# Two-layer decoder trunk on one core: another order for the loads at the start, for the memory attention's projections and for the branch inputs of the merge

## The chip, the cores and the metric

The kernel runs on one core of a Trainium2 chip. The metric is device microseconds of one execution. Before the change three runs took 1638.13, 1638.89 and 1640.25 us; the median is 1638.89 us. One further execution was profiled.

## The reference, cut to what matters

The program computes two layers of a post-norm decoder on x (1024 tokens by 1024 channels, float32). In each layer one projection of x feeds four token mixers, each mixer is gated and projected, and the four are merged. In short form:

```python
h = x @ w_in
(c_q, c_kv, k_rope, sb_qkv, fox_qkv, fox_f, mem_q, gate_z, merge_r) = _split_last(h, IN_SPLITS)
q  = (_rms_norm(c_q, q_norm) @ w_qb)            # branch 0: latent attention with rotary part
kv = (_rms_norm(c_kv, kv_norm) @ w_kvb)
y_mla = causal_softmax(q, kv)
y_sb  = stick_breaking(sb_qkv)                  # branch 1
y_fox = causal_softmax(fox_qkv, log_decay)      # branch 2
mk, mv = jnp.split(mem @ w_mem_kv, 2, axis=-1)  # branch 3: 256 memory tokens
y_mem = softmax((mem_q / 8) @ mk.T) @ mv
merge_g = sigmoid(merge_r @ w_merge_up)
for n in range(4):
    yb = branches[n] * silu(gate_z[:, :, n])
    merged = merged + merge_g[:, :, n] * (yb @ w_branch[n])
x = layer_norm(ALPHA * x + merged @ w_out)
```

## The kernel before, in words

**Numbers in two parts.** Every operand of a large product is split in a high part (float32r) and the rest, its low part, and a product is three matmuls: high by high, low by high, high by low (`passes`, L235 to L237). So each tensor that TensorE reads has a step ahead of it in which one engine writes the high part and another the low part. For activations that is `split_evac`: ScalarE copies (L145, with a scale L148) and VectorE subtracts (L146, with a scale L149). For weights it is `split_pool` on GpSimd (L154 and L157). A tile is 128 by 512, and a projection of the 1024 tokens is done in two halves of 512.

**Weights.** `Stream` takes blocks of 128 by 128 out of one long array in the order that `weight_blocks` lays down; four blocks are one DMA (`wr`, three buffers) and one pair of split tiles (`wh`, `wl`, four buffers each).

**Operands of attention.** `stack_pair` writes a projection's result for two heads into two tiles, opA and opB: ScalarE writes half of opA from PSUM, VectorE the other half out of PSUM and that half (L281, L282), and then the same for opB.

**Order.** The Python code is one program, and a scheduler of the framework puts each engine's instructions in an order of its own, with a simulated timeline. `after(later, earlier)` (L118) only pins an order. Each engine then runs its list strictly in that order, and so does SyncE (SP), which issues the loads. PSUM tiles come from three pools; four banks (`PJ`) serve the projections, and a projection waits until the reader of the bank's last result is done.

**Stages around the change.** At the start of layer 0, x arrives transposed: eight tiles `xr` for the first half of the tokens, taking turns with eight `wAr`, then small tensors, then eight `xr` for the second half. The first product (`pA`, 292 columns: the latent, the rotary key and the forget gate) runs over 8 blocks of tokens. After the first three attentions comes the memory stage: `mem_prep` loads mem, splits it (`memh`, `meml`) and projects keys and values (`mk`, `mv`, matmuls of 256 columns) for two pairs of heads, woven with `cq_norm` (sums of squares for the norm of c_q, `ssp`, L747); then comes the query projection of pair 0. In the gate and latent stage the last gates are projected (`last_gates`), the merge input mr is split (`split_mr`), the gated output of branch 2 is split (`split_y`, tiles `ybh` and `ybl`), the norm weights for q are loaded (`load_wq`), and the latent is transposed (`ckT`), split (`ckTh`, `ckTl`) and projected to keys (`mla_k`) and values (`mla_v`). There `main` holds this list of steps, and `early` feeds in the first steps of the merge (`pg`, `pb`, `mg`, `acc`).

## Time and profile before

| | us |
|---|---|
| median of three runs | 1638.89 |
| profiled execution | 1637.25 |
| its span in the profile | 1635.5 |
| TensorE matmul (PE) busy | 1577.1 (96%) |
| VectorE (DVE) busy | 1057.4 (65%) |
| ScalarE (ACT) busy | 739.4 (45%) |
| GpSimd (POOL) busy | 828.3 (51%) |

PE is busy nearly all the time, and the others about half. So what counts is where PE waits, and where its granted clock is half: the mean granted clock is 0.986 of full. In a row of a timeline, "[1.71 <-DVE xTl L146]" says that the engine stood idle for 1.71 us before this instruction and that VectorE's write of xTl at line 146 ended it. A stretch of a table by windows has, per engine, its busy time and in brackets how many instructions touched it. PEclk is the granted clock, 1.00 for 2.4 GHz and 0.50 for 1.2 GHz.

### The profile page before, as it was taken

The page shows a single profiled execution, that of the slowest core. Times are in us where ns is not written, and L with a number is a line of the kernel's source. Part 1 is how long each engine was busy: PE and PEld are TensorE (multiplying, and loading weights), DVE is VectorE, ACT ScalarE, POOL GpSimd, SP SyncE. Part 2 cuts the span into 40 slices and gives each one's busy share as a digit, 9 for nine tenths or more (in the row PEclk, how much of TensorE's full clock was granted, in tenths as well). Part 3 has the DMA queues.
Part 4 walks back from the last instruction along what each step waited for, and adds up shares of the span by engine and source line. Part 5 has one row for each costly group of instructions (what it writes and reads, how often), then busy time and mean ns, then how long its engine had stood idle before and what let it go on. Part 6 is the DMA issues. An engine that isn't in the chain of part 4 may idle for free. (4 is left out here: it accounts for less than half of the span.)

```text
span 1635.5 us, 24787 instructions
## 1 busy us (share of the span) xinstructions
PE 1577.1 (96%) x8454; PEld 1338.6 (82%) x8454; DVE 1057.4 (65%) x2053; ACT 739.4 (45%) x1632; POOL 828.3 (51%) x971
## 2 busy tenths in 40 slices
PE   9999999999999999989899999999999999999995
PEld 8888888888878888868798888888888788887784
DVE  6456699734436789962673567997343467899618
ACT  4355655534434656420333556655343346564202
POOL 5775535665462344454446664356564623355325
PEclk9999999999999999999899999999999999999998
DMA  5312112232242222132212221122322412221213
GB/s 178 110 56 62 42 36 71 78 88 64 82 127 65 69 71 78 46 116 93 108 68 91 62 59 49 36 64 78 94 66 80 134 56 72 62 84 53 96 65 115
DMA packets 84333, 127.92 MB, mean 78 GB/s; under 512 B 13232, under 2 KB 38640, under 8 KB 84208
## 3 DMA queue, kind: packets, MB, share of 16 engines
q1 hardware_dynamic: 84208, 126.34, 24.9%
q8 instruction: 67, 1.10, 0.3%
q14 instruction: 58, 0.48, 0.1%
HBM read 89.57 MB, written 19.96 MB: 67 GB/s over the span
## 5 line engine op out<-in xcount | busy, mean ns | idle before, releaser
L235 PE MATMUL pj<-xTh,wh 128*128 128x512 f32 x832 | 330.1, 397 | 2.2 <-DVE mx L399 1.4
L237 PE MATMUL pj<-xTh,wl 128*128 128x512 f32 x832 | 326.3, 393 | 0.0
L236 PE MATMUL pj<-xTl,wh 128*128 128x512 f32 x832 | 325.9, 392 | 0.0
L154 POOL TENSOR_SCALAR wh<-wr 128x512 fp32r<-128x512 f32 x168 | 113.9, 678 | 234.5 <-PE pj L236 104.1
L157 POOL TENSOR_TENSOR wl<-wr,wh 128x512 fp32r<-128x512 f32 x168 | 227.1, 1353 | 9.8
L146 DVE TENSOR_TENSOR pl<-pt,ph 128x384 fp32r<-128x384 f32 (+1 forms) x272 | 170.7, 639 | 70.7 <-ACT ph L145 68.3
L145 ACT CAST ph<-pt 128x384 fp32r<-128x384 f32 (+1 forms) x272 | 146.4, 551 | 132.8 <-PE pt L430 128.1
L411 POOL TENSOR_SCALAR p<-p,sm 128x896 f32<-128x896 f32 (+7 forms) x128 | 102.2, 799 | 169.7 <-DVE sm L410 169.3
L237 PEld LDWEIGHTS pj<-xTh,wl 128*128 128x128 f32 x832 | 156.3, 188 | 32.1
L235 PEld LDWEIGHTS pj<-xTh,wh 128*128 128x128 f32 x832 | 156.6, 188 | 29.0 <-DVE mx L399 1.8
L236 PEld LDWEIGHTS pj<-xTl,wh 128*128 128x128 f32 x832 | 156.5, 188 | 26.0
L125 ACT ACTIVATE p<-p,mx 128x896 f32<-128x896 f32 (+7 forms) x128 | 99.4, 777 | 66.9 <-DVE mx L399 57.6
L460 PE MATMUL y<-pl,v 128*128 128x256 f32 (+1 forms) x544 | 121.4, 303 | 0.0
L460 PE MATMUL y<-ph,v 128*128 128x256 f32 (+1 forms) x544 | 111.4, 283 | 1.8 <-ACT ph L145 1.7
L235 PE MATMUL pb<-ybh,wh 128*128 128x512 f32 x256 | 104.3, 407 | 9.0 <-DVE mg L1041 5.4
L430 PE MATMUL pt<-ident_r,p 128*128 128x128 f32 x704 | 110.7, 273 | 0.0
L125 ACT ACTIVATE mg<-pg 128x512 f32<-128x512 f32 x128 | 76.2, 595 | 65.6 <-PE pg L237 40.1
L460 PEld LDWEIGHTS y<-ph,v 128*128 128x128 f32 x544 | 93.2, 189 | 15.0 <-ACT ph L145 3.0
L404 DVE TENSOR_TENSOR_SCAN kt<-kt,unseen 128x896 f32<-128x896 f32 (+3 forms) x64 | 98.0, 1543 | 10.0 <-ACT kt L125 9.8
L237 PE MATMUL po<-woh,mgl 128*128 128x512 f32 x256 | 100.8, 395 | 0.0
L391 POOL TENSOR_SCALAR_AFFINE_SELECT bt<-bt 128x128 f32<-128x128 f32 x64 | 53.0, 831 | 94.1 <-ACT bt L125 85.2
L236 PE MATMUL po<-wol,mgh 128*128 128x512 f32 x256 | 100.5, 396 | 0.0
(266 smaller groups left out, 3692.2 us busy)
## 6 DMA issues: line engine op xcount, KB each, us to landing
wr<-in_w_s_dram SPq DMA_DIRECT2D x168, 256.0 KB, 2.6
s<-opA SPq DMA_DIRECT2D x128, 64.0 KB, 2.0
s<-opB SPq DMA_DIRECT2D x128, 64.0 KB, 2.0
wr<-in_w_out_dram SPq DMA_DIRECT2D x32, 256.0 KB, 2.6
xr<-in_x_t_dram SPq DMA_DIRECT2D x16, 256.0 KB, 5.3
ckb<-c_d SPq DMA_DIRECT2D x8, 512.0 KB, 3.8
y_d<-y SPq DMA_DIRECT2D x16, 256.0 KB, 2.0
y<-y_d SPq DMA_DIRECT2D x16, 256.0 KB, 3.6
```

What stands on the lines that cost most here:

```text
L125: i = act.activation(*args, **kw)
L145: act.copy(h, src)
L146: return dve.tensor_tensor(l, src, f(h), ALU.subtract)
L154: i = pool.tensor_scalar(h, src, 1.0, 1.0, ALU.mult, ALU.mult)
L157: pool.tensor_tensor(l, src, f(h), ALU.subtract)
L235: pe.matmul(ps, ah, bh, start=k == 0, stop=False)
L236: pe.matmul(ps, ah, bl, start=False, stop=False)
L237: pe.matmul(ps, al, bh, start=False, stop=k == nk - 1)
L404: dve.tensor_tensor_scan(kt[:, ::-1], kt[:, ::-1], unseen[:, S - w:][:, ::-1], 1.0, ALU.mult, ALU.max)
L411: pool.tensor_scalar(p, p, sm, 1.0, ALU.mult, ALU.mult)
L430: pe.transpose(pt[:, c:c + P], self.p[i][:, b * P:(b + 1) * P], ident)
L460: pe.matmul(u.y[:, q0 * P:256], u.op["v"][b][:, u.head, :], src[:, s * 256 + q0 * P:s * 256 + 256], start=j == 0 and n == 0, stop=j == n_c ...
```

## The change

Four edits. At the start, the small loads and the first four weight tiles are pinned behind the last load of the second half of x. In the memory stage, the query projection of pair 0 goes first, with the splits of mem and the sums of squares woven in, and the memory's keys and values follow; the weight array has its blocks in the new order. The merge input is split straight out of PSUM when it is projected, and no longer copied and split later. In the latent stage the splits of branch 2 and the load of q's weights are steps of `main` between the latent's and the keys' projections.

```diff
--- before.py
+++ after.py
@@ -196,6 +196,7 @@
         dve.tensor_tensor(dst, dst, t, ALU.mult)
 
     xT = {}
+    last_load = [None]
 
 
     def transpose_x(half, tiles):
@@ -211,7 +212,9 @@
     def wload(n):
 
         raw = rp.tile([P, HALF], F32, tag="wr", name=nm("wr"))
-        nc.sync.dma_start(raw, w_s[n])
+        i = nc.sync.dma_start(raw, w_s[n])
+        if n < 4:
+            after(i, last_load[0])
         wh = hp.tile([P, HALF], F32R, tag="wh", name=nm("wh"))
         wl = hp.tile([P, HALF], F32R, tag="wl", name=nm("wl"))
         split_pool(raw, wh, wl)
@@ -526,7 +529,7 @@
     def load_x(half, k):
 
         raw = U("xr", F32)
-        nc.sync.dma_start(raw, x_t[k * P:(k + 1) * P, half * HALF:(half + 1) * HALF])
+        last_load[0] = nc.sync.dma_start(raw, x_t[k * P:(k + 1) * P, half * HALF:(half + 1) * HALF])
         return raw
 
     def split_x(half, k, raw):
@@ -572,7 +575,7 @@
 
 
     pos_i = cp.tile([P, NB], I32, name="pos_i")
-    nc.sync.dma_start(pos_i, positions.rearrange("o (b p) -> p (o b)", p=P), allow_slow_non_contiguous=True)
+    after(nc.sync.dma_start(pos_i, positions.rearrange("o (b p) -> p (o b)", p=P), allow_slow_non_contiguous=True), last_load[0])
     pos_f = cp.tile([P, NB], F32, name="pos_f")
     inv = cp.tile([P, 16], F32, name="inv")
     freqs = (10000.0 ** (-np.arange(0, ROPE, 2, dtype=np.float64) / ROPE)).astype(np.float32)
@@ -635,7 +638,7 @@
 
 
         fb = tp.tile([P, 4], F32, tag="fb", name=nm("fb"), bufs=1)
-        nc.sync.dma_start(fb, fox_forget_bias[layer].partition_broadcast(P))
+        after(nc.sync.dma_start(fb, fox_forget_bias[layer].partition_broadcast(P)), last_load[0])
         for h in range(4):
             dve.tensor_scalar(fn[:, :, h], fn[:, :, h], fb[:, h:h + 1], 1.0, ALU.add, ALU.mult)
         lf = tp.tile([P, NB, 4], F32, tag="lf", name=nm("lf"), bufs=1)
@@ -713,14 +716,15 @@
         mr = [None, None]
 
         def evac_mr(ps, half):
-            mr[half] = U("mr", F32)
-            act.copy(mr[half], ps)
+            h, l = U("mrh"), U("mrl")
+            split_evac(ps, h, l)
+            mr[half] = (h, l)
 
 
         gq = tp.tile([P, 3], F32, tag="gq", name=nm("gq"), bufs=1)
         gk = tp.tile([P, 2], F32, tag="gk", name=nm("gk"), bufs=1)
-        nc.sync.dma_start(gq, mla_q_norm[layer].rearrange("(k p) -> p k", p=P), allow_slow_non_contiguous=True)
-        nc.sync.dma_start(gk, mla_kv_norm[layer].rearrange("(k p) -> p k", p=P), allow_slow_non_contiguous=True)
+        for g, src in ((gq, mla_q_norm), (gk, mla_kv_norm)):
+            after(nc.sync.dma_start(g, src[layer].rearrange("(k p) -> p k", p=P), allow_slow_non_contiguous=True), last_load[0])
 
         sq = [None, None]
         rq = tp.tile([P, NB], F32, tag="rq", name=nm("rq"), bufs=1)
@@ -745,6 +749,7 @@
             ps = PT("ssp")
             for b in range(NB):
                 pe.matmul(ps[:, 2 * b:2 * b + 1], sq[b // 4][:, (b % 4) * P:(b % 4) * P + P], ones[:, 0:1], start=True, stop=True)
+                yield
             dve.tensor_scalar(ss, ps[:, 0:16].rearrange("p (b t) -> p b t", t=2)[:, :, 0], 1.0 / QR, 1e-6, ALU.mult, ALU.add)
             yield
             rsqrt(rq, ss, NB)
@@ -753,19 +758,25 @@
 
         mo = [{}, {}]
 
-        def mem_prep():
-            memT = []
-            raws = []
+        memT = []
+        mem_raws = []
+
+        def load_mem():
             for k0 in range(0, KT, 2):
                 raw = U("memr", F32).rearrange("p (k c) -> p k c", k=2)
                 nc.sync.dma_start(raw, mem_t[k0 * P:(k0 + 2) * P, :].rearrange("(k p) c -> p k c", p=P))
-                raws.append(raw)
-            for raw in raws:
+                mem_raws.append(raw)
+
+        def split_mem():
+            for raw in mem_raws:
                 h, l = U("memh"), U("meml")
                 split_evac(raw.rearrange("p k c -> p (k c)"), h, l)
                 for k in range(2):
                     memT.append((h[:, k * 256:(k + 1) * 256], l[:, k * 256:(k + 1) * 256]))
-            yield
+                yield
+            mem_raws.clear()
+
+        def mem_prep():
             for pair in range(2):
                 w = st.take(KT)
                 ps = PJ("mk")
@@ -823,8 +834,9 @@
             mo[pair]["q"] = two_halves()
         run(units(sb[1], "sb"), chain(cq_proj(), proj(evac_mr)), 58)
         table("natural_log_exp_and_others")
-        drain(weave(mem_prep(), cq_norm(), 4))
-        drain(proj(stack_pair(mo[0]["q"], SC64)))
+        load_mem()
+        drain(weave(proj(stack_pair(mo[0]["q"], SC64)), chain(split_mem(), cq_norm()), 1))
+        drain(mem_prep())
         table("exp_and_others")
         for pair in range(2):
             mo[pair].update(new_op())
@@ -1006,12 +1018,6 @@
 
         acc = {}
         merged = {}
-
-        def split_mr():
-            for half in range(2):
-                h, l = U("mrh"), U("mrl")
-                split_evac(mr[half], h, l)
-                mr[half] = (h, l)
 
         def merge(n, first, final, following):
             if (n, 0, 0) not in yb:
@@ -1068,16 +1074,11 @@
         side = last_gates()
         while next(side) != 1:
             pass
-        split_mr()
-        split_y(2, 0)
-        split_y(2, 1)
-        load_wq()
-
         def step(f):
             f()
             yield
 
-        main = chain(mla_ckvT(), mla_k(0), mla_k(1), step(lambda: load_cq(1)), mla_v(0), mla_v(1),
+        main = chain(mla_ckvT(), step(lambda: split_y(2, 0)), mla_k(0), step(lambda: split_y(2, 1)), mla_k(1), step(load_wq), step(lambda: load_cq(1)), mla_v(0), mla_v(1),
                      split_cq(1), step(lambda: load_cq(0)), mla_qpe(1), split_cq(0), mla_q(1), mla_qpe(0), mla_qpT(1), mla_q(0), mla_qpT(0))
 
         def early():
@@ -1199,10 +1200,10 @@
             res += tile_of(w_in, base + 256 * i + pair * P)
     for c0 in (0, P, 2 * P, MR0):
         res += tile_of(w_in, c0)
+    res += tile_of(w_in, MQ0)
     for c0 in (0, 256, P, 256 + P):
         res += tile_of(w_mem, c0)
-    for pair in range(2):
-        res += tile_of(w_in, MQ0 + pair * P)
+    res += tile_of(w_in, MQ0 + P)
     for n in (2, 1, 0, 3):
         for pair in range(2):
             res += tile_of(w_in, GZ0 + n * 256 + pair * P)
```

On SP, at the start of the program, the issues before (xr are tiles of x, wr of weights, fb, gq and gk small vectors):

```order
L543 DMA wAr_153<-in_w_a_dram 128x292
L575 DMA pos_i<-in_positions_dram 128x8x1
L214 DMA wr_257<-in_w_s_dram 128x512
L214 DMA wr_263<-in_w_s_dram 128x512
L638 DMA fb_579<-in_fox_forget_bias_dram 128x4
L722 DMA gq_639<-in_mla_q_norm_dram 128x3x1
L723 DMA gk_640<-in_mla_kv_norm_dram 128x2x1
L214 DMA wr_644<-in_w_s_dram 128x512
L529 DMA xr_219<-in_x_t_dram 128x512
```

And now, from the same last wAr on:

```order
L546 DMA wAr_153<-in_w_a_dram 128x292
L532 DMA xr_219<-in_x_t_dram 128x512
L532 DMA xr_221<-in_x_t_dram 128x512
L532 DMA xr_223<-in_x_t_dram 128x512
L532 DMA xr_225<-in_x_t_dram 128x512
L532 DMA xr_227<-in_x_t_dram 128x512
L532 DMA xr_229<-in_x_t_dram 128x512
L532 DMA xr_231<-in_x_t_dram 128x512
L532 DMA xr_233<-in_x_t_dram 128x512
L578 DMA pos_i<-in_positions_dram 128x8x1
L215 DMA wr_257<-in_w_s_dram 128x512
L215 DMA wr_263<-in_w_s_dram 128x512
```

Seven issues, three of them of 256 KB of weights, stand behind the eight of x now. The lists of the other engines are the same at the start.

On PE, at the beginning of layer 0's memory stage, before (y is the last attention's output, ssp the sums of squares, mk and mv the memory's keys and values):

```order
L460 MATMUL y_4317<-ph_3912,v_3136 128x128
L747 MATMUL ssp_3997<-ones,sq_3275 128x1 x4
L747 MATMUL ssp_3997<-ones,sq_3379 128x1 x4
L460 MATMUL y_3856<-pl_3869,v_3150 128x128
L460 MATMUL y_3856<-pl_3869,v_3150 128x256
L460 MATMUL y_4317<-pl_3913,v_3136 128x128
L460 MATMUL y_4317<-pl_3913,v_3136 128x256
L235 MATMUL mk_3986<-memh_3958,wh_3820 128x256
L235 MATMUL mv_4046<-memh_3958,wh_3976 128x256
L236 MATMUL mk_3986<-meml_3959,wh_3820 128x256
```

And now, within the query projection (pj, with x as moving operand):

```order
L751 MATMUL ssp_4007<-ones,sq_3379 128x1
L238 MATMUL pj_4027<-xTh_404,wh_3820 128x512
L239 MATMUL pj_4027<-xTl_405,wh_3820 128x512
L240 MATMUL pj_4027<-xTh_404,wl_3821 128x512
L751 MATMUL ssp_4007<-ones,sq_3379 128x1
```

and at its end:

```order
L239 MATMUL pj_4027<-xTl_425,wh_3826 128x512
L240 MATMUL pj_4027<-xTh_424,wl_3827 128x512
L238 MATMUL mk_4082<-memh_3978,wh_3964 128x256
L239 MATMUL mk_4082<-meml_3979,wh_3964 128x256
L240 MATMUL mk_4082<-memh_3978,wl_3965 128x256
L238 MATMUL mk_4082<-memh_3978,wh_3964 128x256
```

The 48 matmuls of the query projection stand ahead of the first mk, each ssp behind three of them, and the keys are done before the values instead of taking turns with them.

On ACT, in layer 0's latent stage, before (VectorE has the low parts in the same order, behind its own gate):

```order
L125 ACTIVATE gate_5463<-pj_5438 128x512
L145 CAST mrh_5468<-mr_3916 128x512
L145 CAST mrh_5472<-mr_3947 128x512
L148 ACTIVATE ybh_5476<-y_1252 128x512
L148 ACTIVATE ybh_5480<-y_2092 128x512
L148 ACTIVATE ybh_5484<-y_1231 128x512
L148 ACTIVATE ybh_5488<-y_2071 128x512
L148 ACTIVATE ckTh_5521<-ckT_5516,gk_640 128x512
L148 ACTIVATE ckTh_5534<-ckT_5529,gk_640 128x512
L148 ACTIVATE ckTh_5546<-ckT_5541,gk_640 128x512
L148 ACTIVATE ckTh_5558<-ckT_5553,gk_640 128x512
L876 CAST kpe_5570<-kpT_5565 128x512
```

And now, up to the keys' opA and opB and the second pair of ybh:

```order
L148 ACTIVATE ckTh_5514<-ckT_5509,gk_640 128x512
L888 CAST kpe_5526<-kpT_5521 128x512
L888 CAST kpe_5536<-kpT_5531 128x512
L148 ACTIVATE ybh_5541<-y_1252 128x512
L148 ACTIVATE ybh_5545<-y_2092 128x512
L125 ACTIVATE gate_5562<-pj_5481 128x512
L284 ACTIVATE opA_5583<-pj_5552 64x512
L284 ACTIVATE opB_5584<-pj_5552 64x512
L284 ACTIVATE opA_5602<-pj_5589 64x512
L284 ACTIVATE opB_5603<-pj_5589 64x512
L148 ACTIVATE ybh_5608<-y_1231 128x512
L148 ACTIVATE ybh_5612<-y_2071 128x512
```

The two mrh and the four ybh no longer stand between the gate and the ckTh; the ybh stand in two pairs, before the keys' four opA and opB of pair 0 and behind them. In PE's list the two kpT stand side by side now, behind ten more matmuls of the gate than before.

## Rows read from the trace of the kernel before

**Rows 1.** The profile's page, part 1 (busy us, share of the span, instructions) and the granted clock of part 2 in 40 slices.

```profile
PE 1577.1 (96%) x8454; PEld 1338.6 (82%) x8454; DVE 1057.4 (65%) x2053; ACT 739.4 (45%) x1632; POOL 828.3 (51%) x971
...
PEclk9999999999999999999899999999999999999998
```

**Rows 2.** What PE waited for in the whole span: us in total, how often, the longest.

```profile
PE pb L235 <- DVE mg L1041: 5.4, 12, 1.1
PE ckT L865 <- DVE ckTl L149: 4.8, 2, 2.4
...
PE pb L235 <- ACT mg L125: 1.9, 2, 0.9
...
PE pA L237 <- DVE xTl L146: 1.7, 1, 1.7
...
PE pg L235 <- DVE opB L282: 0.9, 2, 0.5
PE mk L236 <- DVE meml L146: 0.8, 3, 0.3
...
PE mk L235 <- ACT memh L145: 0.5, 1, 0.5
```

**Rows 3.** PE's timeline at the start of layer 0: start and duration in us, the instruction, and the idle time before it.

```profile
20.27 0.29 PE L235 MATMUL pA<-wAh,xTh 128*128 128x292 f32 x1
20.41 0.30 PE L236 MATMUL pA<-wAl,xTh 128*128 128x292 f32 x1
22.41 0.40 PE L237 MATMUL pA<-wAh,xTl 128*128 128x292 f32 x1 [1.71 <-DVE xTl L146]
```

**Rows 4.** DVE's timeline there.

```profile
17.90 1.34 DVE L628 CUSTOM_DVE_ANT_0 junk<-ckv 128x256 f32<-128x256 f32 x1
...
19.35 1.33 DVE L628 CUSTOM_DVE_ANT_0 junk<-ckv 128x256 f32<-128x256 f32 x1
...
20.61 2.95 DVE L146 TENSOR_TENSOR xTl<-xr,xTh 128x512 fp32r<-128x512 f32 x3
...
23.65 0.41 DVE L628 CUSTOM_DVE_ANT_0 junk<-ckv 128x256 f32<-128x256 f32 x1
```

**Rows 5.** POOL's timeline there.

```profile
15.75 1.78 POOL L154 TENSOR_SCALAR wh<-wr 128x512 fp32r<-128x512 f32 x3
17.50 4.31 POOL L157 TENSOR_TENSOR wl<-wr,wh 128x512 fp32r<-128x512 f32 x3
```

**Rows 6.** ACT's timeline there.

```profile
18.95 1.86 ACT L145 CAST xTh<-xr 128x512 fp32r<-128x512 f32 x3 [0.91 <-DMA xr<-in_x_t_dram]
```

**Rows 7.** SP's timeline there: when loads were issued.

```profile
9.71 0.38 SPq L575 DMA_DIRECT2D pos_i<-in_positions_dram  x1
...
13.47 4.56 SPq L529 DMA_DIRECT2D xr<-in_x_t_dram  x8
```

**Rows 8.** Windows in the memory stage, of layer 0 (the first four) and of layer 1 (the last): length, then busy us and number of instructions of PE, PEld, DVE, ACT, POOL, then PEclk, the DMA engines' busy share and GB/s.

```profile
320.44:322.19 1.75, 1.75 (x18) 1.75 (x18) 0.00 (x0) 0.45 (x2) 1.50 (x2) 1.00 0.94 324
322.79:324.99 2.20, 1.46 (x9) 0.95 (x8) 0.70 (x2) 0.73 (x3) 0.00 (x0) 0.81 0.85 298
324.99:330.92 5.93, 5.93 (x28) 5.93 (x28) 2.55 (x7) 2.48 (x4) 3.04 (x4) 0.50 0.03 12
330.92:338.00 7.08, 7.08 (x58) 6.99 (x58) 2.11 (x5) 2.21 (x6) 5.96 (x7) 1.00 0.39 113
1137.80:1143.97 6.17, 5.48 (x38) 4.87 (x39) 4.46 (x8) 3.21 (x6) 3.04 (x3) 1.00 0.32 113
```

**Rows 9.** The page's part 5, the splits of weights on POOL: count, busy us, mean ns of one, and idle time before them.

```profile
L154 POOL TENSOR_SCALAR wh<-wr 128x512 fp32r<-128x512 f32 x168 | 113.9, 678 | 234.5 <-PE pj L236 104.1
L157 POOL TENSOR_TENSOR wl<-wr,wh 128x512 fp32r<-128x512 f32 x168 | 227.1, 1353 | 9.8
```

**Rows 10.** Windows in the latent stage of layer 0, columns as in rows 8.

```profile
471.23:474.02 2.79, 0.40 (x3) 0.01 (x1) 2.79 (x5) 0.00 (x0) 2.79 (x5) 1.00 0.00 0
474.02:478.00 3.98, 3.98 (x15) 3.35 (x16) 1.58 (x3) 1.37 (x2) 3.63 (x8) 0.57 0.47 136
490.00:496.31 6.31, 4.91 (x23) 3.65 (x22) 5.13 (x9) 3.38 (x8) 1.29 (x1) 1.00 0.53 146
```

**Rows 11.** DVE's timeline in that stage.

```profile
469.79 3.51 DVE L149 SCALAR_TENSOR_TENSOR ybl<-y,ybh 128x512 fp32r<-128x512 f32 x4
473.22 1.40 DVE L149 SCALAR_TENSOR_TENSOR ckTl<-ckT,gk,ckTh 128x512 fp32r<-128x512 f32 x2
...
492.13 0.69 DVE L282 SCALAR_TENSOR_TENSOR opB<-pj,opB 64x512 fp32r<-64x512 f32 x1 [0.66 <-ACT opB L281]
```

**Rows 12.** ACT's timeline in that stage.

```profile
467.77 2.20 ACT L148 ACTIVATE ybh<-y 128x512 fp32r<-128x512 f32 x4
469.86 1.25 ACT L148 ACTIVATE ckTh<-ckT,gk 128x512 fp32r<-128x512 f32 x2
...
481.64 0.59 ACT L876 CAST kpe<-kpT 128x512 fp32r<-128x512 f32 x1 [3.91 <-PE kpT L874]
```

**Rows 13.** PE's timeline in that stage, two matmuls of a gate's projection.

```profile
478.40 0.39 PE L237 MATMUL pj<-xTh,wl 128*128 128x512 f32 x1
478.63 0.39 PE L235 MATMUL pj<-xTh,wh 128*128 128x512 f32 x1
```

**Rows 14.** A window at the change from layer 0 to layer 1, columns as in rows 8.

```profile
804.00:818.00 14.00, 9.29 (x36) 7.99 (x37) 9.86 (x17) 5.94 (x14) 7.08 (x7) 0.63 0.54 182
```

## The prediction

> **What bounds the kernel now.** I read the page first: PE is busy for 96% of the span and no engine besides TensorE for more than two thirds, and the granted clock falls in two of the 40 slices only [rows 1]. So an edit is worth what it takes from PE's idle time, or from its time at half clock. The second view is what PE waited for [rows 2]. Three places of it lie where the change works: pA behind xTl (1.7 us, the start), mk behind meml and memh (0.8 and 0.5 us, the memory stage of both layers), and ckT behind ckTl (4.8 us in two waits of 2.4 us, one per layer). The longest sum, pb behind mg (5.4 us in 12 waits), lies in the merge, which the change leaves as it is. The third view is the windows around these waits, since a wait is followed by a loss that the waits don't count: in layer 0, 28 matmuls of the memory stage run at a clock of 0.50 and 15 of the latent stage at 0.57 [rows 8, 10].
>
> **Start.** PE has nothing to do between 20.41 and 22.41 us; the wait ended by xTl is 1.71 us [rows 3]. Two things hold xTl back. The eight loads of x were issued from 13.47 us, and ACT waited for the first of them until 18.95 us, 5.5 us later [rows 6, 7]. And DVE reached xTl only at 20.61 us, because two sums over ckv took 1.34 and 1.33 us, while POOL was splitting the first three weight tiles, 15.75 to 21.8 us; the next such sum, which no POOL work covers, took 0.41 us [rows 4, 5]. The change treats both. The loads of x move from 13.47 to 9.71 us, so the first is there at about 15.2 us. The small and the weight loads go 4.56 us back (the time that eight issues of x take [rows 7]); a weight load issued at about 14.7 us is usable, by the same 5.5 us, at about 20.2 us. So POOL is idle while DVE does the sums, these shrink by 0.93 + 0.92 = 1.85 us, and xTl starts at about 18.8 us. PE restarted 1.80 us after the first xTl began (22.41 - 20.61), which is then 20.6 us, when it has just run out of work. Of the hole of 1.87 us (2.00 less one matmul's 0.13) about 1.7 goes; POOL then meets the later xTl, which took 0.98 each with POOL beside them (2.95 for three, rows 4), so I take 1.6 us. It would be below nothing only if the weights came too late: before, POOL had three of them split at 21.8 us, now it has them at about 26.4, and at 20.4 us PE still has four blocks of pA before it, 24 matmuls of 0.13 us each [rows 3], some 13 us, which cover that. It can't be above 1.87 us. Once only, since in layer 1 x comes from the chip.
>
> **Memory stage.** In layer 0 the 36 or so matmuls of 256 columns between 322.79 and 330.92 us take 8.13 us [rows 8]. At the spacing of the next window (58 in 7.08 us, 0.122 us each) they would take 4.4 us: 3.7 us lost, to waiting for the splits of mem while the loads land, and then to the half clock. In layer 1 the clock stayed, and 38 matmuls take 6.17 us instead of 4.6: 1.5 us lost [rows 8]. Now 48 matmuls of the query projection, at 0.23 us each [rows 13], go ahead: 11 us under which loads, splits and the small norm work lie, and 11 us in which PE waits for nothing of mem. That is 3.7 + 1.5 = 5.2 us. The sums of squares (1.75 us for their 16 records, one load of weights each [rows 8]) are woven in now. A lone short matmul still needs its own weight load and then that of its neighbour, so I count no gain there; at most it is 1.75 us per layer. The new wait is for POOL: a pair of splits is 0.68 + 1.35 = 2.03 us [rows 9], and the eight weight tiles of mk and mv last 8 x 12 x 0.122 = 11.7 us on PE at full clock but 16.2 us on POOL. The four buffers let POOL run ahead under the query projection: three tiles are ready or nearly so when mk begins, and the fourth starts when the projection lets its last tile go. The remaining five or so at 2.03 us end about when PE wants the last. It comes out even to within a tile, so I take nothing off, and as the lower bound one tile's 2.0 us in each layer. The term is 5.2 us, between 5.2 - 4.0 = 1.2 and 5.2 + 3.5 = 8.7 us. The splits of mr go under the end of the projections, where DVE and ACT are not waited for; two copies of 0.6 us less per layer lie on ACT, which is 45% busy: nothing.
>
> **Latent stage.** In layer 0 PE does no more than one matmul of the keys from 471.23 us on until 474.02 [rows 10], and of that it is idle for 2.4 us [rows 2]. The two ckTl it waits for ran at 473.22 us, behind four ybl (3.51 us) and, before those, two mrl [rows 10, 11]. With those out of the way ckTl follows the gate, and the hole is gone, with the half clock behind it (3.98 us at 0.57, of which 1.7 us is lost): 4.1 us per layer to be had. But the splits don't vanish. They stand now between kpe and the keys' opA and opB, and there the stage was already paced by ACT and DVE: from kpe at 481.64 to the end of the last opB at 492.82 it is 11.2 us of ACT and DVE in turns [rows 11, 12], and PE lost 1.4 us behind it between 490.00 and 496.31 [rows 10]. Now kpT stands behind ten more gate matmuls. From 471.23 us, 30 matmuls of 0.23 and the ckT transposes of 0.9 us lead to kpe at about 479 us, 2.5 us sooner than before. To the 11.2 us come two pairs of splits, 4 x 0.55 = 2.2 us on ACT (2.20 for four, rows 12) or 4 x 0.69 to 0.88 = 2.8 to 3.5 us on DVE [rows 11]. So the last opB ends between 0.3 us sooner and 1.0 us later than before. PE, which comes earlier to the same work, waits for banks there: the projections of pair 1, pg and v each need a bank that an opB or a gate still reads, and pb's bank frees behind mg; before, such waits by opB and by ACT's mg were 0.9 and 1.9 us in both layers [rows 2]. Followed by hand through the order, these waits sum to about 5.6 us, against the 5.5 us (4.1 and 1.4) lost before, and the state that PE had at 496.31 us is reached some 0.85 us sooner. I take 0.85 us per layer, 1.7 us in all. It would be 8.2 us if the holes were gone and nothing took their place; on the other side 1.0 us per layer for the later opB, and what a fallen clock costs (below). Behind it the mla stage's order is shuffled a little, worth either sign.
>
> **Sum.** 1.6 + 5.2 + 1.7 = 8.5 us from the profiled 1637.25 (its span of 1635.5 and 1.75 around it, which stays) is 1628.75 us; the median of the runs was 1.6 us above the profiled execution, so 1630.4, rounded 1630 us. The rivals' times below are taken from the median, 1638.89.
>
> **Rivals.** First, the latent stage gives its whole hole: 1.6 + 5.2 + 8.2 = 15.0 us, 1623.9. For it speaks that before, only 1.4 us of idle time stood behind the evacuations; against it, that ACT and DVE take 2 us more there. Second, POOL becomes the bound in the memory stage and the latent stage gives nothing: 1.6 + 1.2 + 0 = 2.8 us, 1636.1. For it speaks the 16.2 against 11.7 us; against it the four tiles of head start. Third, the change doesn't do at the start what it says, because the loads of x land no sooner or DVE still meets POOL: 6.9 us, 1632.0, all else as forecast. For it speaks that the DMA engines carry the same bytes in that stretch; against it, that the eight loads of x pass three weight tiles of the same size. The fourth ends on the other side. The 5.6 us of waits in the latent stage come in seven pieces spread over some 13 us, and the clock falls there. Rows show that it falls after short waits too: in layer 0's memory stage it was half from 324.99 us on, after waits that were each about half a microsecond, and it stayed half for 5.93 us, which costs 3.0 us; at the change of layers it was 0.63 over 14 us, so (1 - 0.63) x 2 x 14 = 10.4 us at half, which costs 5.2 us if PE is busy [rows 8, 14]. With the opB 1.0 us later, the latent stage becomes a loss of 4.0 to 6.2 us per layer, and the sum 6.8 - 8.0 to 6.8 - 12.4: 1.2 to 5.6 us slower, 1640.1 to 1644.5. It decides from a loss of 3.4 us per layer in that stage. The Trainium skill ("TensorE: Matmul & The Clock Gate", "A second HAM failure mode: psum-queue depth-cycling") tells of such a case: a kernel that cycled through PSUM banks idled a little between groups of matmuls, often enough that its clock swung and throughput was lost though each matmul looked right. By that page this rival is the likely one; the rows of the latent stage speak against it so far, since the 1.4 us of bank waits at 490 to 496 us left the clock at 1.00 [rows 10].
>
> **How the numbers follow.** Forecast 0.50, first rival 0.17, second 0.17, third 0.08, fourth 0.08. A measurement of this kernel tells 0.2%, 3.3 us, from no change. The forecast is faster in nearly all its spread (0.47 of 0.50), the first wholly, the second in less than half (0.07), the third mostly (0.07): 0.78. Within 0.2%: 0.03 + 0.09 + 0.01 and half of the fourth's lesser end, 0.02: 0.15. Slower 0.07, for the fourth with a short memory stage. The range of 1623 to 1637 us takes in the first rival and the second, and leaves the fourth out.
>
> **What would show it.** Right: no idle time before pA at 20 us, with the two sums on DVE at 0.4 to 0.6 us; clock 1.00 and no wait by memh or meml in either memory stage; no ckT behind ckTl, and instead waits of pj, pg, pb and v behind opB, mg and gate in the 13 us behind kpT. Wrong: POOL as the releaser of mk or mv; a fall of the clock between 480 and 495 us; an xTl that still ends PE's wait; or waits behind opB that are small, which would be the first rival.

## The result, and the profile after

The changed kernel takes 1624.2 us (median of 4 runs, 1623.9 to 1625.1) against 1638.5 us before in the same set of runs: a ratio of 0.9915, 95% interval 0.9898 to 0.9932. In a later set it was 1623.5 against 1635.0 us, ratio 0.9926, 0.9913 to 0.9939. By the medians it is 14.3 us faster in the one set and 11.5 us in the other. The forecast was 8.5 us faster, 1630 us; the range held the time, and the value that came is that of the first rival, 1623.9 us. The experiments show that it came there by another way.

The page of the changed kernel, part 1 and the granted clock, to be set beside [rows 1]:

```profile
PE 1568.6 (97%) x8454; PEld 1331.2 (82%) x8454; DVE 1051.3 (65%) x2053; ACT 738.1 (45%) x1628; POOL 823.5 (51%) x971
...
PEclk9999999999999999999999999999999999999998
```

What PE waits for in it, to be set beside [rows 2]:

```profile
PE pb L238 <- DVE mg L1047: 5.4, 12, 1.1
...
PE pb L238 <- ACT mg L125: 3.2, 5, 0.7
...
PE pj L238 <- DVE gate L804: 2.8, 2, 1.4
...
PE pg L238 <- DVE opB L285: 1.9, 4, 0.6
...
PE pj L238 <- DVE opB L285: 0.8, 2, 0.4
PE v L238 <- DVE opB L285: 0.7, 2, 0.3
```

The waits of pA behind xTl, of mk behind meml and memh and of ckT behind ckTl are gone from the list. Those of the merge (pb behind mg) are as they were. New are pj behind a gate, and pj and v behind opB; pg behind opB and pb behind ACT's mg have grown.

Where the time went can be read by setting the two profiled executions (1637.25 and 1625.05 us, 12.2 us apart) against each other at equal work: the moment at which PE has streamed the same number of columns. The last two columns are the step in what is saved, and what was forecast for it.

```text
stage that ends there          before    after    saved   step   forecast
start, pA                        33.45    31.88    1.57   +1.6    +1.6
first attentions                320.03   319.53    0.51   -1.1     0
memory stage, layer 0           381.23   375.82    5.41   +4.9    +3.7
up to the gates                 461.42   456.03    5.39    0.0     0
latent stage: before its end    479.56   469.93    9.62   +4.2
latent stage, its end           508.15   502.68    5.47   -4.2    +0.85 (both)
mla stage                       610.17   603.30    6.88   +1.4     0
tail, change of layers          844.35   835.91    8.44   +1.6     0
memory stage, layer 1          1203.34  1192.53   10.81   +2.4    +1.5
latent stage, layer 1          1329.92  1319.23   10.69   -0.1    +0.85
mla stage, layer 1             1501.68  1489.48   12.20   +1.5     0
end                            1611.87  1599.62   12.25    0.1     0
```

Two of the steps belong to the granted clock, and no run ties them to one of the edits. The -1.1 us before the memory stage is a fall of the clock at about 203 us (below). The +1.6 us at the change of layers stands beside a clock of 0.91 and 0.86 in the windows 705 to 725 and 790 to 815 us, where it was 0.83 and 0.81 before. The run with the start alone has 0.83 and 0.80 there and a step of 0.0 us, the run with the memory stage alone 0.91 and 0.86 and a step of 1.8 us, though neither edit touches that stretch.

**Start.** DVE of the changed kernel there, to be set beside [rows 4], and then POOL, beside [rows 5]:

```profile
18.10 0.42 DVE L631 CUSTOM_DVE_ANT_0 junk<-ckv 128x256 f32<-128x256 f32 x1
...
18.66 0.41 DVE L631 CUSTOM_DVE_ANT_0 junk<-ckv 128x256 f32<-128x256 f32 x1
...
19.00 1.90 DVE L146 TENSOR_TENSOR xTl<-xr,xTh 128x512 fp32r<-128x512 f32 x3
```

POOL, its first split of a weight tile:

```profile
22.54 1.16 POOL L154 TENSOR_SCALAR wh<-wr 128x512 fp32r<-128x512 f32 x1 [6.35 <-DMA wr<-in_w_s_dram]
```

The two sums take 0.42 and 0.41 us instead of 1.34 and 1.33, and xTl begins at 19.00 us instead of 20.61. POOL gets its first weights only at 22.5 us, two microseconds later than I had worked out.

**Memory and latent stage.** Windows of the changed kernel, columns as in [rows 8]: the query projection, the keys and values of the memory behind it, and the latent stage.

```profile
322.50:331.50 9.00, 9.00 (x49) 7.68 (x48) 5.29 (x9) 4.63 (x8) 1.91 (x2) 1.00 0.26 90
332.32:346.00 13.68, 13.68 (x114) 13.59 (x113) 4.18 (x8) 3.77 (x9) 11.84 (x14) 1.00 0.53 155
...
474.00:491.00 17.00, 12.39 (x59) 8.71 (x58) 10.16 (x15) 10.31 (x19) 8.42 (x15) 1.00 0.31 108
```

In the memory stage PE has no idle time and the full clock; POOL is busy for 11.84 of 13.68 us and keeps up. In the latent stage PE is idle for 4.6 of 17 us, and ACT and DVE are busy for 10 each. The idle time there, on PE's timeline:

```profile
477.64 0.50 PE L238 MATMUL pj<-ckTh,wkvh 128*128 128x512 f32 x1 [1.38 <-DVE gate L804]
...
479.71 0.50 PE L238 MATMUL pj<-ckTh,wkvh 128*128 128x512 f32 x1 [0.42 <-DVE opB L285]
...
481.93 0.47 PE L238 MATMUL pg<-mrh,wh 128*128 128x512 f32 x1 [0.56 <-DVE opB L285]
...
483.60 0.50 PE L238 MATMUL pb<-ybh,wh 128*128 128x512 f32 x1 [0.75 <-ACT mg L125]
...
485.59 0.36 PE L238 MATMUL v<-wkvh,ckTh 128*128 128x256 f32 x1 [0.34 <-DVE opB L285]
```

These are the waits that were forecast, in the forecast order. The 2.4 us hole and the half clock of [rows 10] are gone, 4.2 us are saved by 470 us, and all of it is given back by 508 us.

**A clock fall that comes and goes.** In the step of -1.1 us before the memory stage the granted clock falls for a while. The changed kernel in its first profile:

```profile
198.00:212.00 14.00, 12.98 (x61) 10.28 (x60) 12.34 (x17) 8.81 (x22) 4.39 (x6) 0.88 0.15 47
```

And in its second profile, taken with the later set:

```profile
198.00:212.00 14.00, 12.98 (x75) 10.72 (x73) 13.39 (x17) 10.59 (x26) 4.80 (x7) 1.00 0.17 50
```

It is the same program with the same waits (three of them, 1.0 us together, in each), 0.88 in the one and 1.00 in the other. So a comparison of two single executions carries an error of this size: the step of -1.1 us before the memory stage is -0.05 us in the second profile.

### The profile page after: what moved, and what is told of

Read it like the earlier page. It is cut to its first block, busy times and chain, and to the rows that moved or that the text cites. A ratio compares the mean times of both kernels' runs of the same rounds, so it can differ in the third digit from the quotient of the medians.

```text
span 1623.3 us, 24793 instructions
## 1 busy us (share of the span) xinstructions
PE 1568.6 (97%) x8454; PEld 1331.2 (82%) x8454; DVE 1051.3 (65%) x2053; ACT 738.1 (45%) x1628; POOL 823.5 (51%) x971
## 5 line engine op out<-in xcount | busy, mean ns | idle before, releaser
L463 PEld LDWEIGHTS y<-ph,v 128*128 128x128 f32 x544 | 92.0, 189 | 11.3 <-ACT ph L145 1.6
```

The lines of the kernel that those rows point to most:

```text
L463: pe.matmul(u.y[:, q0 * P:256], u.op["v"][b][:, u.head, :], src[:, s * 256 + q0 * P:s * 256 + 256], start=j == 0 and n == 0, stop=j == n_c ...
```

## Experiments: each edit alone

**The start alone.**

```diff
+        i = nc.sync.dma_start(raw, w_s[n])
+        if n < 4:
+            after(i, last_load[0])
...
+    after(nc.sync.dma_start(pos_i, ...), last_load[0])
...
```

> The kernel before with the new load order at the start alone. Theory (as forecast, 1.6 us): the 1.71 us wait of pA behind xTl is gone, the two sums on DVE take 0.4 to 0.7 us, and the time falls by 1.6 us, so about 1.0 to 2.0 us. Rival: the clock fall of 3.4 us at 203 us in the profile of the changed kernel is a consequence of this edit, then it stands in this profile too and the net is 0 to 0.5 us. If the fall is chance, it is in some profiles of any kernel and has nothing to do with the edit.

Measured: 1632.8 against 1635.6 us, ratio 0.9984 (0.9972 to 0.9996), 2.6 us with 0.7 to 4.6. The wait behind xTl is gone from its profile, and the clock was 1.00 from 198 to 212 us. The forecast 1.6 us lies inside. The rival (the fall is the edit's work) can't be refuted by one profile without the fall, since the fall comes and goes; but the run with the merge input alone (below), which has the old order of loads, shows the fall too, so it doesn't need this edit:

```profile
198.00:212.00 14.00, 12.97 (x62) 10.31 (x61) 12.37 (x16) 7.68 (x19) 4.31 (x6) 0.88 0.18 47
```

**The memory stage alone.**

```diff
-        drain(weave(mem_prep(), cq_norm(), 4))
-        drain(proj(stack_pair(mo[0]["q"], SC64)))
+        load_mem()
+        drain(weave(proj(stack_pair(mo[0]["q"], SC64)), chain(split_mem(), cq_norm()), 1))
+        drain(mem_prep())
...
```

> The kernel before with the memory stage's edit alone (query projection first, weight blocks in the new order). Theory (forecast): 5.2 us less, 3.7 in layer 0 and 1.5 in layer 1. The traces of before and after set against each other say 4.9 and 2.4, 7.3 us; if the edit alone accounts for this, the time falls by about 7 us, and no clock fall stands between 320 and 350 us. Rival: part of it is lent by the other edits (the copy of mr gone, the start's shift), then 5 us or less.

Measured: 1627.1 against 1635.6 us, ratio 0.9948 (0.9931 to 0.9965), 8.5 us with 5.7 to 11.3. It is the largest part, and it needs none of the other edits. Set against the profile before at equal work it saves 4.9 us in layer 0's memory stage and 2.3 in layer 1's, as the changed kernel does. The rival falls.

How the 7.3 us are shared between the layers hangs on the one execution of before. The run with the latent stage's order alone (below) keeps the old memory stage, and yet it is 2.2 us ahead in layer 0's, with a clock of 1.00 where the kernel before had 0.87 (the first window), and 1.6 us behind in layer 1's, with 0.89 from 1130 to 1146 us where the kernel before had 1.00. Each of the four profiles with the old memory stage has a fall of the clock in that stage of one layer or of both, none of the ten with the new one has any.

```profile
320.00:346.00 26.00, 25.46 (x168) 22.48 (x167) 7.24 (x17) 8.17 (x18) 19.52 (x20) 1.00 0.45 142
...
462.00:474.00 12.00, 9.61 (x47) 7.67 (x46) 9.19 (x11) 5.56 (x10) 11.03 (x16) 1.00 0.27 86
```

The second window is of this run, the memory stage alone, in layer 0's latent stage. The hole of 2.4 us behind ckTl is there as before, but the clock stayed at 1.00, which saved 1.6 us at equal work. So a hole of this length isn't always followed by half the clock.

**The merge input alone.** Only this edit: mr is split out of PSUM when it is projected.

```diff
-            mr[half] = U("mr", F32)
-            act.copy(mr[half], ps)
+            h, l = U("mrh"), U("mrl")
+            split_evac(ps, h, l)
+            mr[half] = (h, l)
...
-        split_mr()
```

> The kernel before with the merge input split from PSUM, and nothing else. Theory A (as forecast): nothing, since ACT and DVE are not waited for where the split lands, and the four ybl still stand ahead of ckTl. Theory B, read from the DVE rows: the two mrl (2.39 us) are most of the 2.40 us by which ckTl comes late, so without them the hole in the latent stage shrinks to 0.5 us or less and the half clock goes with it; 2.4 + 1.7 us in each layer, 6 to 8 us in all.

Measured: 1629.5 against 1635.6 us, ratio 0.9965 (0.9950 to 0.9980), 5.7 us with 3.3 to 8.2. Theory B holds and theory A, my forecast, falls. The row of DVE before on which theory B rests, directly ahead of the four ybl of [rows 11]:

```profile
467.48 2.39 DVE L146 TENSOR_TENSOR mrl<-mr,mrh 128x512 fp32r<-128x512 f32 x2
```

DVE of this run in the latent stage:

```profile
465.96 3.89 DVE L149 SCALAR_TENSOR_TENSOR ybl<-y,ybh 128x512 fp32r<-128x512 f32 x4
469.77 1.40 DVE L149 SCALAR_TENSOR_TENSOR ckTl<-ckT,gk,ckTh 128x512 fp32r<-128x512 f32 x2
```

And PE there, its only wait behind ckTl in layer 0:

```profile
470.56 0.65 PE L866 MATMUL ckT<-ident_r,ckv 128*128 128x128 f32 x4 [0.40 <-DVE ckTl L149]
```

The four ybl still stand ahead of ckTl. But the two mrl (2.39 us of DVE before) are not there, so the hole is 0.40 us instead of 2.40 us, and at equal work 3.6 us are saved by the middle of layer 0's stage, of which 3.0 stay at its end, and 2.7 us in layer 1's.

**The latent stage's order alone.**

```diff
-        split_y(2, 0)
-        split_y(2, 1)
-        load_wq()
...
-        main = chain(mla_ckvT(), mla_k(0), mla_k(1), step(lambda: load_cq(1)), ...
+        main = chain(mla_ckvT(), step(lambda: split_y(2, 0)), mla_k(0), step(lambda: split_y(2, 1)), mla_k(1), step(load_wq), ...
```

> The kernel before with branch 2's splits and q's weight load moved into the list of the latent stage, and nothing else; mr is still split at that stage's beginning. Theory: the hole of 2.4 us goes and comes back as waits of pj, pg, pb and v behind opB, mg and gate, some 5 to 6 us per layer, as in the changed kernel; net between 0 and 2 us less, or a little more with the two mrl still there. Rival: the mla stage behind it, where the changed kernel gained 1.5 us per layer, is this edit's work; then 3 us less in all, gained behind 500 us and not in the stage.

Measured: 1635.5 against 1635.6 us, ratio 0.9997 (0.9988 to 1.0006): no change. At equal work 4.3 us are gained up to 473 us and 5.0 lost by 494 (the clock's fall below is in it), and about 1.5 us are gained in the mla stage of each layer. In this run the fourth rival shows itself too: the clock falls in the middle of the waits (a window, columns as in [rows 8]).

```profile
483.00:487.00 4.00, 3.68 (x11) 2.52 (x10) 2.81 (x5) 3.07 (x6) 4.00 (x9) 0.57 0.26 73
```

## Experiments: one part undone

**The changed kernel again**, as the measure for the next three kernels and in one set with them.

> The changed kernel as it is, on the chip of the next three, so that these can be set against it. Expected: 11 to 14 us below the kernel before. If the clock fall at 203 us of its first profile is chance, it is not in this profile, or stands elsewhere.

Measured: 1623.5 us (1621.5 to 1623.7), 11.5 us below the kernel before. No fall at 203 us (the second of the two windows above).

**The latent stage's order undone.** Branch 2's splits and the load of q's weights stand ahead of `main` again; the rest is the changed kernel.

```diff
+        split_y(2, 0)
+        split_y(2, 1)
+        load_wq()
...
+        main = chain(mla_ckvT(), mla_k(0), mla_k(1), step(lambda: load_cq(1)), ...
```

> The changed kernel with one part undone: branch 2's splits and q's weight load stand ahead of the latent's transposes again, as before the change; mr is split from PSUM as in the change. Theory (from the run with mr alone): no hole over 0.5 us at ckT, since the two mrl are gone, no waits of 5 us behind opB and mg, 2.5 to 3 us less per layer in the latent stage; against it the 1.4 us per layer that the mla stage gained by the other order. So 2 to 3 us faster than the changed kernel. Rival: moving the splits is what cured the hole in the changed kernel, then it is back, with the half clock, and this is 6 to 8 us slower than the changed kernel.

Measured: 1620.8 us (1618.0 to 1623.1), ratio 0.9908 (0.9895 to 0.9922): 2.7 us below the changed kernel by the medians. The two intervals overlap, but four of the five runs lie below all five of the changed kernel, and the traces agree: at equal work, against the changed kernel's first profile, this one gains 2.9 us in layer 0's latent stage and gives back 0.6 us behind it, and 3.0 and 0.9 us in layer 1. So the fourth edit costs time.

**The weights ahead of x again.**

```diff
-        if n < 4:
+        if n == 3:
             after(i, last_load[0])
```

> The changed kernel with one part undone: the first three weight tiles are loaded ahead of the second half of x again, as before; only the four small loads stay behind it. x is issued from about 11.7 us and there at about 17.2 us, sooner than DVE can use it, so only POOL's splits beside the sums on DVE are as before. Theory (DVE): the sums take 1.3 us again, xTl starts at about 20.6 us, and the wait of pA of 1.5 to 1.7 us is back: 1.5 us slower than the changed kernel. Rival (arrival of x): the wait is gone though POOL is busy, and the time is that of the changed kernel.

Measured: 1626.1 us (1625.3 to 1627.0), 2.6 us above the changed kernel. DVE in it:

```profile
17.66 1.34 DVE L631 CUSTOM_DVE_ANT_0 junk<-ckv 128x256 f32<-128x256 f32 x1
...
19.10 1.33 DVE L631 CUSTOM_DVE_ANT_0 junk<-ckv 128x256 f32<-128x256 f32 x1
...
20.36 2.95 DVE L146 TENSOR_TENSOR xTl<-xr,xTh 128x512 fp32r<-128x512 f32 x3
```

And PE:

```profile
22.16 0.40 PE L240 MATMUL pA<-wAh,xTl 128*128 128x292 f32 x1 [1.71 <-DVE xTl L146]
```

x is there in time (ACT begins its copies at 17.70 us and waits for no load), and the wait is 1.71 us, to the hundredth that of before. So here not the arrival of x held PE, but DVE, which POOL's splits slowed. That a later POOL alone would have been enough isn't shown: with x as late as before (ACT's first copy at 18.95 us, 0.62 us each [rows 6]) xTl could not have begun before about 19.6 us, against 19.00 in the changed kernel.

## Experiments: a better place, and the pace of the stage

**Branch 2's splits a stage earlier.**

```diff
-        finish(chain(gate(0, 0), gate(0, 1)), 2)
+        finish(chain(gate(0, 0), step(lambda: split_y(2, 0)), gate(0, 1), step(lambda: split_y(2, 1))), 2)
...
-        main = chain(mla_ckvT(), step(lambda: split_y(2, 0)), mla_k(0), step(lambda: split_y(2, 1)), mla_k(1), step(load_wq), ...
+        main = chain(mla_ckvT(), mla_k(0), mla_k(1), step(load_wq), ...
```

> The changed kernel with branch 2's splits moved to the stage before, between the two gates of branch 0 (around 430 to 460 us), where ACT and DVE are busy for a third of the time or less. Theory: with the splits out of the chain of opA and opB, that chain is 3 us shorter, the waits of pj, pg, pb and v behind it fall from 5.9 us per layer to about 3, and nothing holds ckTl: 4 to 6 us faster than the changed kernel. Rival: the chain of opA and opB alone paces the stage, and PE arrives at it the sooner, so the waits stay at 5 us and the time within 2 us of the changed kernel.

Measured: 1622.7 us (1618.8 to 1624.5), ratio 0.9922 (0.9909 to 0.9934): 0.9 us below the changed kernel, not told apart from it by these runs. The stage did about what was expected: in the profile PE's waits in layer 0's stage fall from 4.6 us (not 5.9, as the expectation had it) to 2.7, and the stage gains 2.6 us in each layer at equal work. But the mla stage behind it gives back 1.3 us of that in each. The profiled run is also the fastest, 1618.8 us at a mean granted clock of 0.994; the five others had 0.989 to 0.993.

**The pace of the evacuations.** In `stack_pair` ACT writes its half of opA, DVE its half, and only then ACT its half of opB. This kernel lets ACT write both first:

```diff
             for t, r0 in ((a, 0), (b, 64)):
+                act.activation(t[r0:r0 + 64, :], ps[r0:r0 + 64, :], AF.Copy, scale=scale)
+            for t, r0 in ((a, 0), (b, 64)):
                 lo = 64 - r0
-                act.activation(t[r0:r0 + 64, :], ps[r0:r0 + 64, :], AF.Copy, scale=scale)
```

> The changed kernel, but each evacuation writes both of ACT's halves (opA, opB) first and DVE's halves after them, so that ACT no longer waits for DVE within a pair (everywhere stack_pair is used). Theory (the chain paces): one pair takes two DVE steps, about 1.4 us, instead of 2.13 us, four pairs 3 us less; the waits of pj, pg, pb and v in the latent stage fall from 5.9 us to about 3 us per layer, and the time by 4 to 6 us below the changed kernel. Rival: the waits are set by the gate and the splits of branch 2 between the pairs, then they stay at 5 us and the time within 1.5 us of the changed kernel.

Measured: 1626.9 us, ratio 0.9958 (0.9943 to 0.9973), slower than the changed kernel. In the latent stage it gained 2.6 us in layer 0, as expected, but at the head of the list of what PE waited for stands a new one:

```profile
PE sc L345 <- DVE opB L286: 7.2, 8, 2.4
```

In the attentions before that stage the scores now wait for DVE's half of opB; why it comes later there wasn't followed up. The same edit on the two other kernels:

> The kernel with the latent stage undone (splits of branch 2 ahead of the latent's transposes, mr from PSUM) and the evacuation order of the run before. Theory: the stage's remaining waits there (0.9 behind opB at the transposes of rq, 0.6 and 1.2 at pg and pb) fall by half or more; 2 to 3 us below the same kernel with the old evacuation order, 1617 to 1619, the fastest of all. Rival: the time stays at 1621.

Measured: 1624.0 us, ratio 0.9930 (0.9914 to 0.9945); the wait of 7.2 us is there too, and the expected 1617 to 1619 is missed.

> The changed kernel with branch 2's splits between the two gates of branch 0, and the new evacuation order. Theory: neither splits nor ACT's waits are in the chain, so PE's waits in the latent stage fall from 3.4 us to under 1.5 us per layer; 1616 to 1619. Rival: the waits are then behind mg (pb), which neither edit touches, and the time is that of the run before within 1.5 us.

Measured: 1624.4 us, ratio 0.9936 (0.9919 to 0.9953); the wait of 7.2 us is there again, and 1616 to 1619 is missed. So the last run uses the order only for the latent's keys, on the kernel with the latent stage undone:

```diff
...
-                stack_pair(ml[pair]["k"], 1.0)(ps, half)
+                stack_pair(ml[pair]["k"], 1.0, True)(ps, half)
...
```

> The kernel with the latent stage undone (as e6), and the new evacuation order for the latent's keys alone, so that the attentions before keep theirs. In e9 to e11 that order gained 1.2 to 2.5 us per layer in the latent stage and lost 5 to 7 us in waits of the scores behind opB elsewhere. Theory: here only the gain stays, 1.2 to 1.6 us per layer: 2 to 3 us below e6, 12 to 15 us more below the kernel before than nothing, so a ratio of 0.989 to 0.990, and no wait of sc behind opB. Rival: the waits go over to pb behind mg, and the ratio is that of e6, 0.991.

Measured: 1618.6 us (1617.5 to 1620.2), ratio 0.9900 (0.9882 to 0.9917), the fastest by the median. No wait of sc behind opB is left, and ACT's halves follow each other. The first row is of the same kernel with the old order, where ACT stood 0.75 us idle before the second half; the two others are of this run:

```profile
475.57 0.59 ACT L284 ACTIVATE opB<-pj 64x512 fp32r<-64x512 f32 x1 [0.75 <-DVE opA L285]
...
473.85 0.59 ACT L284 ACTIVATE opA<-pj 64x512 fp32r<-64x512 f32 x1
474.45 0.60 ACT L284 ACTIVATE opB<-pj 64x512 fp32r<-64x512 f32 x1
```

PE is idle for 2.1 us with the old order (first row) and for 1.1 with the new one, in the window in which the changed kernel was idle for 4.6:

```profile
474.00:491.00 17.00, 14.95 (x83) 12.25 (x82) 11.34 (x19) 9.00 (x18) 6.16 (x6) 1.00 0.42 126
...
474.00:491.00 17.00, 15.86 (x87) 13.13 (x86) 11.66 (x19) 9.11 (x18) 5.75 (x5) 1.00 0.41 124
```

All its runs lie below all of the changed kernel's, in both sets. Against the kernel with the stage undone and the old order it is 2.2 us by the medians, but the intervals overlap; that step isn't shown. In the traces the order of the keys gains 1.0 and 1.5 us in the two latent stages, and 0.8 us is lost again in each mla stage.

## Why the prediction was right in sign and short in size

In the first pair of traces 12.25 us were saved and 8.5 forecast. The memory stage gave 2.1 us more than forecast, the mla stages 2.9 and the falls of the clock 0.5, and the latent stage 1.7 less.

- **Start: right, and by the right cause.** 1.6 us forecast, 1.57 in the traces, 2.6 (0.7 to 4.6) alone. That the traces agree to some hundredths is luck: from 20.2 to 24 us the changed kernel gains 2.0 us at equal work in both its profiles, a little above the 1.87 us that I called the most, and in the first it had lost 0.4 us before that. Of the two causes that I named, the run with the weights first shows POOL's splits beside DVE's sums to be enough to hold PE. The earlier issue of x alone brought nothing; whether it was needed beside the other isn't shown. The third rival falls.
- **Memory stage: mechanism right, size short.** The hole and the half clock went, POOL kept up, and the second rival didn't come. 5.2 us forecast, 7.3 in the traces, 8.5 (5.7 to 11.3) alone. The term counted the 36 and 38 matmuls only. Of the 2.1 us that it lacks, 0.9 us is a wait of y behind ACT's ph in the stage that follows: 1.7 us in four waits before, 0.8 in two after, and 0.8 in two in the run with the memory stage alone. The rest isn't assigned; that the last attention's products, which stood between the sums of squares and mk, have a part in it isn't shown. The 8.5 us of the run alone hold 7.3 within their interval. Weaving the sums brought nothing, as forecast. PE's timeline after:

```profile
322.93 0.28 PE L751 MATMUL ssp<-ones,sq 128*128 128x1 f32 x2
323.06 0.48 PE L238 MATMUL pj<-xTh,wh 128*128 128x512 f32 x1
323.38 0.40 PE L239 MATMUL pj<-xTl,wh 128*128 128x512 f32 x1
323.61 0.39 PE L240 MATMUL pj<-xTh,wl 128*128 128x512 f32 x1
```

  From 322.93 to 323.38 it is 0.45 us instead of a matmul's 0.23: 0.22 us for each of eight pairs of records, 1.8 us against the 1.75 us of before.
- **Latent stage: the waits right, the credit wrong.** That the hole would go and come back as waits behind gate, opB and mg is what the profile shows; 0.85 us per layer was left of it in the forecast, 0.08 and -0.12 in the traces. The 0.85 doesn't follow from the prediction's own sum: waits of 5.6 us in place of 5.5 us lost leave -0.1 us per layer, which is about what came. The step that failed is the sentence that the splits of mr, moved under the projections, are worth nothing. They are worth 5.7 us (3.3 to 8.2) alone. I had the row for it (the two mrl took DVE 2.39 us ahead of ckTl, and the wait was 2.40 us) and gave that to the move of the four ybl. The move itself is worth nothing alone, and in the changed kernel it costs 2.7 us by the medians. The price of 4.1 us per layer, too, had a part that doesn't always come: the clock fell behind the hole in both layers before, but in only one of the two in the run with the start alone and in the run with the memory stage alone. One rival stands untested. DVE's steps in that queue were slow beside POOL, which split q's weights then: the four ybl took 0.88 us each [rows 11], and two of them in the changed kernel 0.65 us each at 475.69 us, where POOL was idle. The edit moved the load of q's weights together with the ybl, and no run moves that load alone.
- **Behind it: not forecast.** The mla stage gained 1.4 and 1.5 us. The run with the order alone gains as much there (1.4 and 1.5), the runs with one of the other edits alone between -0.1 and 0.8 us. The run with the order undone keeps 0.8 and 0.7 us, so that edit's work is only a part of it. The run with the splits a stage earlier has 0.2 us in each layer, though it loads q's weights where the changed kernel does: that part goes with the place of the splits and not with that of the load. Where the rest comes from is open.
- **The rivals.** The first rival's value came true by luck, and not its cause: the latent stage didn't give its hole. The fourth (a clock fall among the bank waits) was in none of the two profiles of the changed kernel, but in that of the order alone (0.57 at 483 us). The page of the Trainium skill that I cited ("TensorE: Matmul & The Clock Gate", "A second HAM failure mode: psum-queue depth-cycling") agrees with that run in this one place, and not with the two of the changed kernel, where PE was idle for 4.6 and 4.5 of 17 us and the clock stayed at 1.00.

## What to carry to other kernels

When several instructions stand ahead of a late one in an engine's queue, compare the wait with each of them alone: here taking out the one that was as long as the wait was enough, and moving the rest only put them into the next chain. An evacuation order that helps one stage can starve another that uses the same helper, so change it for the stage. And load order at a kernel's start is also a matter of what the loads set off on other engines.

## What the runs showed of the hardware

A VectorE sum of 128 by 256 took 0.41 us alone and 1.33 us beside GpSimd's splits, three times as long; xTl took 0.98 us beside them and 0.63 us (1.90 for three) without. And the granted clock from 198 to 212 us was 0.88 in one execution of the changed kernel and 1.00 in another, with equal waits around it: such a fall is no property of the program alone, and here two profiles differ by 1.0 us for it.
